# Stage 1 of a hybrid encoder layer: the normalized input taken by columns from memory, with the row factors spread by two transposes

## The chip, the cores and the metric

The kernel runs on one core of a Trainium2 chip. The metric is the device time of one execution in microseconds. The time before is the median of three runs; the profile is of one further execution.

## The reference

Two sequences (prompt and sample), each of 1024 rows and 1024 columns in fp32, go through one encoder layer. Each has a conditioning vector that modulates the normalized input:

```python
mod = jax.nn.silu(c) @ w_ada + b_ada
sh1, sc1, ga1, sh2, sc2, ga2 = split(mod, 6)
h = rmsnorm(x, g_mix) * (1.0 + sc1) + sh1      # rmsnorm: a factor for each row of x
z = h @ w_in                                   # q_lat 256, kv_lat 128, k_pe 64, f_in 512
y_mla = mla_group(q_lat, kv_lat, k_pe, ...)    # attention on low-rank latents, 4 heads
y_four = real(fft2(f_in)) per group @ w_four   # Fourier mixing
x = x + ga1 * (concat(y_mla, y_four) @ w_out)
h2 = rmsnorm(x, g_ffn) * (1.0 + sc2) + sh2
x = x + ga2 * ((silu(h2 @ w_gate) * (h2 @ w_up)) @ w_down)
y = rmsnorm(x, g_final)
```

Everything that the change touches lies in the first two lines of h and z.

## The kernel before

Every fp32 product is made of three matmuls (mm3, L78 to L80): each operand is split into a rounded part and a rest, by a cast on ACT (L62) and a subtraction on DVE (L63). A name ending in h (hh, eoh, lh) is the rounded part, one ending in l (hl, eol, ll) the rest.

Stage 1, which ends near 230 us, makes z in eight pairs k = 0 to 7, four for each sequence. A pair is two tiles of 128 rows (u = 0 and 1), rows p and p + 512, all 1024 columns. A program that schedules instructions places them; on each engine they then run in the fixed order that it chose, and SyncE's queue of loads and stores is in order too, at most eight under way at a time. For pair k, the code issues these steps:

- x_load(k+2): two loads of 512 KB into xt, the rows on partitions.
- zproj(k, 0): 24 matmuls make the 448 latent columns of tile 0 in a PSUM bank. ACT squares them (L413, L414), POOL makes the latents' row factors (rstd, L103 to L110: rs_v, rs_y, rs_w, rs_r), DVE makes the rotary products t (L420 to L422) and scales the latents into lat (L425, L426), POOL adds t into lat (L424), and the kv part is split and stored (ckv, L431).
- flip(k+1, 0) and flip(k+1, 1): h of the next pair by columns. Eight 128x128 transposes of xt on TensorE (L382) fill two banks; ACT multiplies by 1 + sc1 and adds sh1 (L389, hf; four pieces of 256 for these two flips, a few of pair 0 on DVE, L387), then hf is split into hh and hl, 512 at a time.
- zproj(k, 1), then latents(k, 0): four transposes of lat (L440), split into lh and ll and stored.
- flip(k+1, 2) and flip(k+1, 3): the other half of the columns.
- norm(k+2): ACT squares the rows of xt (L366), POOL makes the row factor rs_r by the same rstd, and DVE multiplies xt by it (L369).
- fourier_in(k, 0): 24 matmuls (F0 below) on the sum of the two tiles; latents(k, 1); evenodd(k+1, 0): POOL adds the two tiles of hf into eo (L400), which is split; fourier_in(k, 1) on the difference; evenodd(k+1, 1).

So zproj and fourier_in of pair k read what flip and evenodd made during pair k-1, and flip(k+1) reads what norm(k+1) made during pair k-1.

Between these steps a generator (extras) hands out other work: fold_out (a product of the output weights, L251, its result so on DVE, L253); eight products of 1 MB of modulation weights for the gates (mod_mm(1, c), L216, c = 0 to 7, "the second set", since the first eight for shift and scale are done before pair 0), each load (wada, L207) issued one step ahead; then gated output weights (L311, with so on DVE, L315). In pair 0 the flips stand behind zproj(0, 1) and among the products of fold_out.

The SBUF pool of the stage holds four xt tiles of 4 KB per partition and one hf tile of 8 KB per partition. The PSUM pool has eight banks, used in turn.

Of the kernel before, what the change touches and what calls it, by code (L numbers as in the profile page):

```python
# [21 lines left out]
P = 128  # L22
# [30 lines left out]
def hybrid_encoder_kernel(ctx: ExitStack, tc: tile.TileContext, a: dict):  # L53
# [109 lines left out]
    with ExitStack() as st:  # L163
# [5 lines left out]
        def bank():  # L169
            return pp.tile([P, 512], F32, tag="b", name="bank")  # L170

        def xtile():
            return w2.tile([P, D], F32, tag="x", name="xt", bufs=4)

# [26 lines left out]
        def wada_tile():  # L201
            return w2.tile([P, 4, 512], F32, tag="wada", name="wada", bufs=2)
# [149 lines left out]
        def x_load(k):  # L352
            s, j = pairs[k]
            st1["x", k] = [xtile() for _ in range(2)]
            for u in range(2):
                nc.sync.dma_start(st1["x", k][u], xs[s][rows(j, u), :])

        def norm(k):
            if ("x", k) not in st1:
                x_load(k)  # L360
            ms = tiny.tile([P, 2], F32, name="ms")
            xt = st1["x", k]
            for u in range(2):
                t = xt[u]
                jk = w.tile([P, D], BF16, tag="junk", name="junk", bufs=1)
                nc.scalar.activation(jk, t, AF.Square, scale=1.0 / 32.0, accum_out=ms[:, u : u + 1])  # L366
            r = rstd(ms, 2)
            for u in range(2):
                nc.vector.tensor_scalar(out=xt[u], in0=xt[u], scalar1=r[:, u : u + 1], scalar2=None, op0=ALU.mult)  # L369

        def flip(k, g):
            s, j = pairs[k]
            if g == 0:
                st1["hf", k] = w2.tile([P, NC, 2, P], F32, tag="hf", name="hf", bufs=1)
                st1["hh", k] = w.tile([P, NC, 2, P], F32R, tag=f"hh{k % 2}", name="hh")
                st1["hl", k] = w.tile([P, NC, 2, P], F32R, tag=f"hl{k % 2}", name="hl")
            hf, xt = st1["hf", k], st1["x", k]
            pt = bank().rearrange("p (c u t) -> p c u t", c=2, u=2)
            for c in range(2):
                for u in range(2):  # L380
                    cc = 2 * g + c
                    nc.tensor.transpose(pt[:, c, u, :], xt[u][:, cc * P : (cc + 1) * P], ident)  # L382
            for c in range(2):
# [95 lines left out]
        def wide(tag, shape=(P, 4, 512)):  # L479
            return (w2 if tag == "hf" else w).tile(list(shape), F32, tag=tag, name="wide")  # L480

# [39 lines left out]
        nc.sync.dma_start(ropes, a["ropes"])  # L521
        x_load(1)
        wpe = w.tile([P, 2, HEADS * ROPE], F32, tag="lh", name="wpe", bufs=2)
        nc.sync.dma_start(wpe, a["wpe"])
        wuvT = w.tile([P, HEADS, KVL], F32, tag="gah1", name="wuvT")
        nc.sync.dma_start(wuvT, a["wuvT"])
        wo2 = wo_load(0, wada_tile().rearrange("p a b -> p (a b)").rearrange("p (a b) -> p a b", a=2))
        mod_mm(0, 6, ch[6])
        wz_split(0, wz0)
# [9 lines left out]
        with behind():  # L539
            fold_pe(wpe, gq)  # L540
        zproj(0, 0)
        norm(1)
        evenodd(0, 1)
        nk = len(pairs)
        more = extras()

        def pair(k, also=None):
            if k + 2 < nk:
                x_load(k + 2)
            if also is not None:  # L550
                also(0)
            if k > 0:
                zproj(k, 0)
            if also is not None:
                with tc.issue_after(here["sq"]):
                    also(1)
            if 0 < k < nk - 1:
                flip(k + 1, 0)
                flip(k + 1, 1)
            next(more, None)  # L560
            zproj(k, 1)
            if k == 0:
                fold_out(0, wo2, wuvT, gq)
                flip(k + 1, 0)
                flip(k + 1, 1)
                fold_out(1, wo2, wuvT, gq)
# [1185 lines left out]
def _layout(i):  # L1752
# [10 lines left out]
    for s in range(2):  # L1763
# [3 lines left out]
    r = {  # L1767
        "x0": sq["x_prompt"][slots], "x1": sq["x_sample"][slots],
        "cT": c.reshape(2, NC, P).transpose(2, 1, 0),
        "w_ada": sq["w_ada"], "bT": b.reshape(48, P).T, "bga": bga,  # L1770
# [30 lines left out]
```

## Time and profile before

| | us |
|---|---|
| three runs | 2043.54, 2043.8, 2045.34 (median 2043.8) |
| the profiled execution | 2044.17 |
| its span, first to last instruction | 2042.3 |
| TensorE busy | 1986.2 (97%) |
| mean granted TensorE clock | 0.993 |

Stage 1 by stretches, each from the end of one pair's first projection to the next's (pair 1 ends its first projection at 85.87):

| stretch, us | length | TensorE busy | DVE | ACT | POOL | DMA share |
|---|---|---|---|---|---|---|
| 0 to 40 | 40.00 | 24.02 | 12.60 | 11.47 | 3.68 | 0.94 |
| 57 to 70 | 13.00 | 8.51 | 7.44 | 8.78 | 11.13 | 0.29 |
| 70 to 85.87 | 15.87 | 15.87 | 12.64 | 8.14 | 5.88 | 0.90 |
| 85.87 to 107.65 | 21.78 | 21.78 | 12.06 | 12.60 | 11.49 | 0.95 |
| 107.65 to 129.43 | 21.78 | 21.78 | 10.96 | 13.78 | 10.91 | 0.76 |
| 129.43 to 150.01 | 20.58 | 20.58 | 13.88 | 12.50 | 10.63 | 0.84 |
| 150.01 to 176.51 | 26.50 | 25.64 | 20.90 | 15.02 | 14.78 | 0.64 |
| 176.51 to 198.80 | 22.29 | 22.29 | 16.40 | 12.64 | 11.53 | 0.55 |
| 198.80 to 230 | 31.20 | 29.89 | 22.32 | 20.22 | 15.17 | 0.41 |

How to read the views: in a group, "a, b | c <-X d" is busy time, the mean in ns of one, and the idle time of that engine ahead of the group with what ended it. In a list of waits, the numbers are total, times and the longest. In a timeline, the numbers are start and duration; matmuls overlap, so their spacing is read from starts. In a row of windows, the columns are the length, busy time and count of TensorE, its weight loads, DVE, ACT and POOL, then the granted clock, the DMA share and GB/s.

### The profile page before, as it was taken

Reading aid. Unit: us, or ns where it says so; the run is one execution under the profiler, and the core shown is the slowest. Engines: PE = TensorE matmul, PEld = TensorE weight load, DVE = VectorE, ACT = ScalarE, POOL = GpSimd, SP = SyncE. Lnnn points to the kernel's source line nnn. Section 1 sums busy time; section 2 is a strip of 40 time slices with the busy share of each in tenths; the row PEclk is TensorE's granted clock in tenths of the full one; section 3 lists DMA queues with packets and bytes.
Section 4 is the critical chain, followed back from the end, with each engine's and each line's share of the span. In section 5 each row is a group of like instructions: output and inputs, shape, how many; then the busy total and the mean of one; then the engine's idle time right before and its main releaser. Section 6 shows DMA issues by size and latency. Waiting matters only on the chain.

```text
span 2042.3 us, 27832 instructions
## 1 busy us (share of the span) xinstructions
PE 1986.2 (97%) x9610; PEld 1629.8 (80%) x9610; DVE 1410.6 (69%) x2082; ACT 897.1 (44%) x1741; POOL 832.8 (41%) x1021
## 2 busy tenths in 40 slices
PE   6999999999999999999999999999999999999997
PEld 4788877888888877888888888877788888888876
DVE  3667757766677668878777676677766665657674
ACT  3655635555465554333333365453333333336441
POOL 0555213111313226879779410332654455410142
PEclk8999999999999999999999999999999999999999
DMA  9785694544643475546655587664423322358662
GB/s 358 237 257 180 224 337 133 126 104 103 160 114 128 125 273 196 191 164 202 202 164 191 179 306 249 215 232 146 140 101 103 109 98 103 113 182 271 231 217 90
DMA packets 183817, 370.30 MB, mean 181 GB/s; under 512 B 19004, under 2 KB 60476, under 8 KB 180604
## 3 DMA queue, kind: packets, MB, share of 16 engines
q1 hardware_dynamic: 165004, 310.72, 46.0%
q0 software_dynamic: 18672, 57.81, 9.5%
q8 instruction: 75, 1.23, 0.3%
q14 instruction: 66, 0.54, 0.1%
HBM read 256.46 MB, written 120.39 MB: 185 GB/s over the span
## 4 chain that ended last, share of the span: by engine, by line
PE 55%; DVE 3%; DMA 1%; POOL 1%; issue 1%; ACT 0%; SPq 0%; DVEq 0%; ACTq 0%; POOLq 0%
PE bank L79 18%; PE bank L78 18%; PE bank L80 18%; DVE wl L63 1%; DMA draw<-s_d 1%; DVE val L138 1%; ACT wh L62 0%; DMA val<-x_d 0%; DVE val L1600 0%; DMA rgu<-in_wgu_dram 0%; POOL val L138 0%; POOL rs_y L106 0%; DMA draw<-t_d 0%; SPq L1559 0%; DVE val L135 0%
## 5 line engine op out<-in xcount | busy, mean ns | idle before, releaser
L78 PE MATMUL bank<-H,wh 128*128 128x512 f32 x1224 | 477.4, 390 | 7.0 <-DVE val L138 6.5
L80 PE MATMUL bank<-H,wl 128*128 128x512 f32 x1224 | 476.5, 389 | 0.2 <-DVE wl L63 0.2
L79 PE MATMUL bank<-H,wh 128*128 128x512 f32 x1224 | 476.2, 389 | 0.0
L138 DVE TENSOR_TENSOR val<-bank,val 128x512 f32<-128x512 f32 x244 | 166.7, 688 | 167.4 <-PE bank L80 166.1
L78 PEld LDWEIGHTS bank<-H,wh 128*128 128x128 f32 x1224 | 229.8, 188 | 58.0 <-DVE val L138 7.7
L80 PEld LDWEIGHTS bank<-H,wl 128*128 128x128 f32 x1224 | 229.8, 188 | 49.1 <-DVE wl L63 1.5
L79 PEld LDWEIGHTS bank<-H,wh 128*128 128x128 f32 x1224 | 229.8, 188 | 47.4
L63 DVE TENSOR_TENSOR wl<-draw,wh 128x512 fp32r<-128x512 f32 x286 | 202.2, 740 | 86.3 <-ACT wh L62 86.0
L62 ACT CAST wh<-draw 128x512 fp32r<-128x512 f32 x286 | 168.9, 620 | 159.9 <-PE bank L79 85.3
L79 PE MATMUL bank<-wl,wh 128*128 128x512 f32 x572 | 223.7, 391 | 4.0 <-DVE wl L63 4.0
L138 POOL TENSOR_TENSOR val<-val 128x512 f32<-128x512 f32 x58 | 83.6, 1449 | 345.5 <-DVE val L1574 191.5
L78 PE MATMUL bank<-wh 128*128 128x512 f32 x572 | 222.7, 389 | 0.4 <-ACT wh L62 0.4
L80 PE MATMUL bank<-wh,wl 128*128 128x512 f32 x572 | 222.7, 389 | 0.0
L62 ACT CAST wh<-rgu 128x512 fp32r<-128x512 f32 x171 | 106.3, 623 | 251.0 <-PE bank L79 192.1
L63 DVE TENSOR_TENSOR wl<-val,wh 128x512 fp32r<-128x512 f32 x133 | 140.4, 1057 | 70.9 <-ACT wh L62 70.7
L63 DVE TENSOR_TENSOR wl<-rgu,wh 128x512 fp32r<-128x512 f32 x171 | 166.6, 975 | 7.3 <-ACT wh L62 7.2
L62 ACT CAST wh<-val 128x512 fp32r<-128x512 f32 x133 | 82.3, 622 | 179.9 <-PE bank L79 158.6
L135 POOL TENSOR_TENSOR val<-rgu 128x512 f32<-128x512 f32 x80 | 113.8, 1422 | 100.0 <-DMA rgu<-in_wgu_dram 96.3
L79 PEld LDWEIGHTS bank<-wl,wh 128*128 128x128 f32 x572 | 107.4, 188 | 29.4 <-DVE wl L63 7.3
L78 PEld LDWEIGHTS bank<-wh 128*128 128x128 f32 x572 | 107.4, 188 | 23.2 <-ACT wh L62 0.9
L80 PEld LDWEIGHTS bank<-wh,wl 128*128 128x128 f32 x572 | 107.4, 188 | 22.2
L135 POOL TENSOR_TENSOR val<-val 128x512 f32<-128x512 f32 x89 | 119.4, 1358 | 1.3
(381 smaller groups left out, 3913.2 us busy)
## 6 DMA issues: line engine op xcount, KB each, us to landing
rgu<-in_wgu_dram SPq DMA_DIRECT2D x86, 512.0 KB
draw<-s_d SPq DMA_DIRECT2D x143, 256.0 KB
s_d<-val POOLq DMA_DIRECT2D x88, 256.0 KB, 3.5
draw<-t_d SPq DMA_DIRECT2D x88, 256.0 KB
s_d<-val SPq DMA_DIRECT2D x66, 256.0 KB
draw<-in_w_down_dram SPq DMA_DIRECT2D x55, 256.0 KB
wada<-in_w_ada_dram SPq DMA_DIRECT2D x13, 1024.0 KB
xt<-in_x_dram SPq DMA_DIRECT2D x16, 512.0 KB
```

The source lines that it names most:

```text
L62: here["a"] = nc.scalar.copy(hi, src).ins
L63: here["v"] = nc.vector.tensor_tensor(out=lo, in0=src, in1=rd(hi), op=ALU.subtract).ins
L78: nc.tensor.matmul(out, lh, rh, start=first, stop=False, skip_group_check=cont)
L79: nc.tensor.matmul(out, lh, rl, start=False, stop=False, skip_group_check=cont)
L80: nc.tensor.matmul(out, ll, rh, start=False, stop=last, skip_group_check=cont)
L135: return eng.tensor_tensor(out=out, in0=x, in1=y, op=ALU.subtract).ins
L138: return eng.tensor_tensor(out=out, in0=x, in1=y, op=ALU.add).ins
```

## The change

From pair 1 on, h by columns no longer comes from transposes of xt. The host also gives x already laid out by columns (xT, 128 partitions of column index, 8 chunks, 2 tiles, 128 rows). A load of 1 MB (xT_load) puts it into hf, of which there are now two; xt is loaded still, for the squares alone, and has two tiles in place of four. The row factor has to multiply along the free axis there, so scale_cols spreads it: two transposes on TensorE of rs_r broadcast along columns (L383) give a 128x256 block in a PSUM bank whose every partition holds the factors of the 256 rows, and two DVE multiplications of 1024 elements (L386) scale hf in place. flip then runs ACT's multiply-add on hf in place (L410) and splits it as before. Pair 0 keeps its path.

Three things move with it. x_load(1) and xT_load(1) are issued behind wpe, wuvT and the first output weights. norm(1) is issued ahead of zproj(0, 0), and evenodd(0, 1) behind norm(1)'s last POOL operation. The load xT(k+2) fills the hf that pair k used, so on SyncE it waits until POOL has read that in evenodd(k, 1).

```diff
-            return w2.tile([P, D], F32, tag="x", name="xt", bufs=4)
+            return w2.tile([P, D], F32, tag="x", name="xt", bufs=2)
...
+        def xT_load(k):
+            s, j = pairs[k]
+            st1["hf", k] = w2.tile([P, NC, 2, P], F32, tag="hf", name="hf", bufs=2)
+            nc.sync.dma_start(st1["hf", k], a[f"xT{s}"][j])
...
             r = rstd(ms, 2)
+            if k > 0:
+                st1["r", k] = r
+                return
             for u in range(2):
                 nc.vector.tensor_scalar(out=xt[u], in0=xt[u], scalar1=r[:, u : u + 1], scalar2=None, op0=ALU.mult)
+
+        def scale_cols(k):
+            hf, r = st1["hf", k], st1.pop(("r", k))
+            pr = bank()[:, :256].rearrange("p (u t) -> p u t", u=2)
+            for u in range(2):
+                nc.tensor.transpose(pr[:, u, :], r[:, u : u + 1].broadcast_to([P, P]), ident)
+            for g in range(2):
+                gs = slice(4 * g, 4 * g + 4)
+                nc.vector.tensor_tensor(out=hf[:, gs], in0=hf[:, gs], in1=pr.unsqueeze(1).broadcast_to([P, 4, 2, P]), op=ALU.mult)
...
-            pt = bank().rearrange("p (c u t) -> p c u t", c=2, u=2)
-            for c in range(2):
-                for u in range(2):
-                    cc = 2 * g + c
-                    nc.tensor.transpose(pt[:, c, u, :], xt[u][:, cc * P : (cc + 1) * P], ident)
+            if k > 0:
+                pt = hf[:, 2 * g : 2 * g + 2]
+            else:
+                pt = bank().rearrange("p (c u t) -> p c u t", c=2, u=2)
+                for c in range(2):
+                    for u in range(2):
+                        cc = 2 * g + c
+                        nc.tensor.transpose(pt[:, c, u, :], xt[u][:, cc * P : (cc + 1) * P], ident)
...
-        x_load(1)
         wpe = w.tile([P, 2, HEADS * ROPE], F32, tag="lh", name="wpe", bufs=2)
...
         wo2 = wo_load(0, wada_tile().rearrange("p a b -> p (a b)").rearrange("p (a b) -> p a b", a=2))
+        x_load(1)
+        xT_load(1)
         mod_mm(0, 6, ch[6])
...
+        with behind():
+            norm(1)
+        placed = here["p"]
         zproj(0, 0)
-        norm(1)
-        evenodd(0, 1)
+        with tc.issue_after(placed):
+            evenodd(0, 1)
...
             if k + 2 < nk:
                 x_load(k + 2)
+                xT_load(k + 2)
...
             if 0 < k < nk - 1:
+                scale_cols(k + 1)
                 flip(k + 1, 0)
                 flip(k + 1, 1)
             next(more, None)
             zproj(k, 1)
             if k == 0:
                 fold_out(0, wo2, wuvT, gq)
+                scale_cols(k + 1)
                 flip(k + 1, 0)
```

The scheduler sets the rest. Two places of its order follow. The first is ACT in pair 2, from the squares of the first projection (L413 and L414, now L434 and L435) to those of the second. Before:

```order
L413 ACTIVATE junk,mz<-bank 128x256
L414 ACTIVATE junk,mz<-bank 128x128
L389 ACTIVATE hf<-bank,sh_0_77,s_0_75 128x256 x3
L62 CAST hh<-hf 128x512
L62 CAST kv<-lat 128x128
L389 ACTIVATE hf<-bank,sh_0_77,s_0_75 128x256
L62 CAST hh<-hf 128x512
L413 ACTIVATE junk,mz<-bank 128x256
```

In the changed kernel, where L410 is what L389 was:

```order
L434 ACTIVATE junk,mz<-bank 128x256
L435 ACTIVATE junk,mz<-bank 128x128
L410 ACTIVATE hf<-hf,sh_0_77,s_0_75 128x256 x3
L62 CAST kv<-lat 128x128
L62 CAST hh<-hf 128x512
L410 ACTIVATE hf<-hf,sh_0_77,s_0_75 128x256 x2
L62 CAST hh<-hf 128x512
L410 ACTIVATE hf<-hf,sh_0_77,s_0_75 128x256 x2
L434 ACTIVATE junk,mz<-bank 128x256
```

Three more hf stand ahead of the second squares, and kv ahead of the first hh.

The second is DVE in pair 6, up to the scaling of the first tile's latents (L425 and L426, now L446 and L447); t_2293, t_2197 and t_2265 are rotary products. Before:

```order
L420 TENSOR_TENSOR t_2293<-bank,ropec 128x64
L421 TENSOR_TENSOR t_2293<-bank,ropes 128x32
L422 TENSOR_TENSOR t_2293<-bank,ropes 128x32
L315 TENSOR_TENSOR so<-bank,gah 128x512
L63 TENSOR_TENSOR hl<-hf,hh 128x512 x2
L425 TENSOR_SCALAR lat<-bank,rs_r 128x256
L426 TENSOR_SCALAR lat<-bank,rs_r 128x128
```

In the changed kernel, behind the three operations of the first tile's t (t_2197); t_2265 is the second tile's:

```order
L386 TENSOR_TENSOR hf<-hf,bank 128x1024 x2
L315 TENSOR_TENSOR so<-bank,gah 128x512 x3
L63 TENSOR_TENSOR hl<-hf,hh 128x512 x2
L441 TENSOR_TENSOR t_2265<-bank,ropec 128x64
L315 TENSOR_TENSOR so<-bank,gah 128x512
L442 TENSOR_TENSOR t_2265<-bank,ropes 128x32
L443 TENSOR_TENSOR t_2265<-bank,ropes 128x32
L63 TENSOR_TENSOR hl<-hf,hh 128x512 x2
L315 TENSOR_TENSOR so<-bank,gah 128x512
L446 TENSOR_SCALAR lat<-bank,rs_r 128x256
L447 TENSOR_SCALAR lat<-bank,rs_r 128x128
```

The first tile's scaling now stands behind both L386, five so, four hl and the second tile's t.

On TensorE, the product of the second set moved too: the one for c = 0 runs behind zproj(1, 0), c = 1 within fourier_in(1, 1), c = 2 within zproj(2, 0), c = 3 within zproj(2, 1), and so on to c = 7 at the start of zproj(4, 0). On SyncE, the loads for c = 1, 2 and 4 stand behind an xT load and the stores of ckv or of the latents that follow it. From the end of pair 6 on, the order on every engine is as before.

More of the change, by code (lines that the diff above doesn't have):

```diff
@@ L373, in flip @@
             if g == 0:
-                st1["hf", k] = w2.tile([P, NC, 2, P], F32, tag="hf", name="hf", bufs=1)
+                if k == 0:
+                    st1["hf", k] = w2.tile([P, NC, 2, P], F32, tag="hf", name="hf", bufs=2)
                 st1["hh", k] = w.tile([P, NC, 2, P], F32R, tag=f"hh{k % 2}", name="hh")
@@ L479, in wide @@
         def wide(tag, shape=(P, 4, 512)):
-            return (w2 if tag == "hf" else w).tile(list(shape), F32, tag=tag, name="wide")
+            if tag == "hf":
+                return w2.tile(list(shape), F32, tag=tag, name="wide", bufs=2)
+            return w.tile(list(shape), F32, tag=tag, name="wide")
         cols0 = [(0, 2048)]
@@ L1768, in _layout @@
         "x0": sq["x_prompt"][slots], "x1": sq["x_sample"][slots],
+        **{f"xT{s}": x[slots].reshape(2, 4, P, NC, P).transpose(1, 4, 3, 0, 2)
+           for s, x in enumerate((sq["x_prompt"], sq["x_sample"]))},
         "cT": c.reshape(2, NC, P).transpose(2, 1, 0),
```

## The prediction

> **What bounds the kernel now.** I read the page first (busy shares and the chain that ended last), then TensorE's waits and line groups in stage 1, then timelines of single pairs.
>
> ```profile
> PE 1986.2 (97%) x9610; PEld 1629.8 (80%) x9610; DVE 1410.6 (69%) x2082; ACT 897.1 (44%) x1741; POOL 832.8 (41%) x1021
> PE 55%; DVE 3%; DMA 1%; POOL 1%; issue 1%; ACT 0%; SPq 0%; DVEq 0%; ACTq 0%; POOLq 0%
> ```
>
> TensorE works 97% of the span: a TensorE instruction taken out is worth its time, unless the next instruction then has to wait. Between 58 and 300 us, TensorE waits only here:
>
> ```profile
> PE bank L382 <- DVE xt L369: 4.5, 1, 4.5
> PE bank L440 <- DVE lat L425: 2.2, 3, 0.9
> PE bank L899 <- DMA wada<-in_w_ada_dram: 1.6, 1, 1.6
> ```
>
> The first is the first wait for a row factor, the second says that the latent chain is already just in time in three pairs. A steady pair on TensorE (pair 1, from the end of its first projection):
>
> ```profile
> 85.67 0.36 PE L80 MATMUL bank<-wz_h,hl 128*128 128x448 f32 x1
> 85.87 1.03 PE L382 MATMUL bank<-ident,xt 128*128 128x128 f32 x8
> 86.83 1.06 PE L216 MATMUL bank<-wada,scT 128*32 128x512 f32 x8
> 87.83 0.48 PE L78 MATMUL bank<-wz_h,hh 128*128 128x448 f32 x1
> 92.77 0.60 PE L440 MATMUL bank<-ident,lat 128*128 128x128 f32 x4
> 93.20 1.04 PE L382 MATMUL bank<-ident,xt 128*128 128x128 f32 x8
> 94.17 1.06 PE L216 MATMUL bank<-wada,scT 128*32 128x512 f32 x8
> 95.17 0.39 PE L78 MATMUL bank<-wcs_h,eoh 128*128 128x280 f32 x1
> ```
>
> By starts, eight transposes take 86.83 - 85.87 = 0.96 and 94.17 - 93.20 = 0.97 us, so 0.12 each; L440 takes 0.43, a 1 MB modulation product (L216) 1.00, the second projection 92.77 - 87.83 = 4.94. The chain beside it, from a projection's end to the scaled latents:
>
> ```profile
> 86.07 0.38 ACT L413 ACTIVATE junk<-bank 128x256 bf16<-128x256 f32 x1 [3.32 <-PE bank L80]
> 86.89 0.22 POOL L103 TENSOR_SCALAR rs_v<-mz 128x2 f32<-128x2 f32 x1 [5.01 <-ACT junk L414]
> 89.04 0.48 DVE L425 TENSOR_SCALAR lat<-bank,rs_r 128x256 f32<-128x256 f32 x1 [1.79 <-POOL rs_r L110]
> 89.44 0.34 DVE L426 TENSOR_SCALAR lat<-bank,rs_r 128x128 f32<-128x128 f32 x1
> ```
>
> 85.87 to 89.78: 3.9 us at best. Before, TensorE has 0.43 + 0.97 + 1.00 + F0 (3.1, the 24 matmuls from 95.17 at 0.13) = 5.5 us between zproj(k,1) and latents(k,1), which covers it.
>
> **The change part by part.** Prices of what it touches, from the line groups up to 340 us:
>
> ```profile
> L382 PE MATMUL bank<-ident,xt 128*128 128x128 f32 x128 | 19.0, 298 | 4.5 <-DVE xt L369 4.5
> L369 DVE TENSOR_SCALAR xt<-xt,rs_r 128x1024 f32<-128x1024 f32 x16 | 11.4, 751 | 12.7 <-POOL rs_r L110 12.7
> L63 DVE TENSOR_TENSOR ll<-bank,lh 128x512 fp32r<-128x512 f32 x16 | 10.9, 685 | 0.3
> L342 DVE TENSOR_TENSOR wcs_l<-bank,wcs_h 128x256 fp32r<-128x256 f32 x16 | 6.4, 421 | 12.5 <-ACT wcs_h L341 12.0
> L389 ACT ACTIVATE hf<-bank,sh,s 128x256 f32<-128x256 f32 x60 | 31.2, 576 | 8.4 <-PE bank L382 8.4
> L62 ACT CAST hh<-hf 128x512 fp32r<-128x512 f32 x32 | 20.0, 628 | 1.4 <-DVE hf L387 1.1
> L62 ACT CAST lh<-bank 128x512 fp32r<-128x512 f32 x16 | 9.2, 583 | 0.0
> ```
>
> Removed: 7 x 16 transposes of xt; added: 7 x 2 of rs_r. That is 14 x 0.12 = 1.69 us less in each of seven pairs, if nothing waits.
>
> L386 in place of L369: no trace has it. Below, L369's 0.75 us for 1024 elements; above, two 512-wide PSUM operations, 2 x 0.685 = 1.37. From 421 ns (256) to 685 (512) the step is 264 per 256 elements, so 685 + 2 x 264 = 1.21 us, which I take. It also stands after the first projection, directly ahead of the hf activations, where L369 was done early. The Trainium skill, "VectorE: DVE Perf Modes", section "Why PSUM operands drop a tier", says that fp32 work with a PSUM operand runs at the single rate while a single-source operation in SBUF can run at twice that. It speaks against this change; by it L386 is nearer 1.2 than 0.75, and at 0.75 the sum below would be about 1 us better, through pairs 1 and 6 alone. hf from SBUF instead of PSUM: hh (SBUF) against lh (PSUM) is 45 ns more at 512, so 0 to 0.05 each, taken as nothing; each runs beside projections.
>
> What stops the gain is the interval. Without the 0.97, and with the modulation product moved into or ahead of the projections, TensorE reaches latents(k,1) 0.43 + 3.1 = 3.5 us after zproj(k,1), against a chain of 3.9. ACT adds to it: in pairs 1 to 3 seven hf, two hh and kv stand ahead of the second squares, where four hf, two hh and kv stood. Starting when L386 and the first squares are through (about 1.6 us after the projection), three hf take 1.4 us, kv waits for lat to 4.0, then kv 0.2, hh 0.5, two hf 0.95, hh 0.5, two hf 0.95: the second squares start at 7.15. Spacings are by starts, a little under the means above.
>
> Pair by pair, after minus before, against the profiled execution:
>
> - Pair 0: the 4.5 us stall is shown by
>
> ```profile
> 65.55 0.41 PE L382 MATMUL bank<-ident,xt 128*128 128x128 f32 x2 [4.49 <-DVE xt L369]
> 62.20 0.22 POOL L103 TENSOR_SCALAR rs_v<-ms 128x2 f32<-128x2 f32 x1
> 64.65 1.42 DVE L369 TENSOR_SCALAR xt<-xt,rs_r 128x1024 f32<-128x1024 f32 x2 [1.31 <-POOL rs_r L110]
> ```
>
>   The factor now comes at about 60, ahead of zproj(0,0)'s own, and 1.9 us of transposes go. In exchange POOL makes lat(0,0) and lat(0,1) behind it and behind two eo, so latents(0,0) waits in its place. fourier_in(0,0) comes at about 70.3 in place of 72.6: -2.4 (bounds -1 to -3.5).
> - Pair 1: L386 is held up behind pair 0's last so (L253) and splits; latents(1,1) waits about 2.0: 2.0 - 1.69 = +0.3. The third modulation product waits 0 to 2 us for its load, which now goes out behind xT(3) and ckv writes; taken 0.3. Together +0.6.
> - Pairs 2 and 3: zproj(k,1) ends at 0.24 + 4.9 + 1.0 = 6.2, squares at 7.15, lat at 10.9; TensorE is there at 9.7 to 9.9. A wait of 1.0 leaves -0.75 each, -1.5.
> - Pair 4: only four hf stand ahead of the squares, and the 0.86 of the latent waits goes: -1.69 - 0.86 = -2.55.
> - Pair 5: lat(5,0) on DVE stands behind work of zproj(5,1): +0.4 after the gain.
> - Pair 6: the largest term. Before:
>
> ```profile
> 198.80 1.03 PE L382 MATMUL bank<-ident,xt 128*128 128x128 f32 x8
> 204.42 0.47 DVE L425 TENSOR_SCALAR lat<-bank,rs_r 128x256 f32<-128x256 f32 x1
> 205.03 0.63 PE L440 MATMUL bank<-ident,lat 128*128 128x128 f32 x4 [0.39 <-DVE lat L425]
> 205.50 1.04 PE L382 MATMUL bank<-ident,xt 128*128 128x128 f32 x8
> ```
>
>   lat(6,0) starts 5.6 us after the projection's end and fourier_in(6,0) 7.6. After, ahead of lat(6,0) on DVE stand two L386 (2.4), five so (5 x 0.6), four hl (2.4) and six small t (0.6), 8.4 us, and the last hl needs an hh that ACT makes only behind the second squares. lat at about 10.8, fourier_in at 11.6: +4.1 (bounds +1 to +5).
> - Pair 7: the latent wait at 227 (0.9) shrinks: -0.8.
>
> The sum is -2.4 + 0.6 - 1.5 - 2.55 + 0.4 + 4.1 - 0.8 = -2.2 us.
>
> The clock: TensorE then stands still about 5.5 us in pair 6. What a stall does to it, in windows of 5 us:
>
> ```profile
> 60.00:65.00 5.00, 1.06 (x3) 0.19 (x1) 2.10 (x7) 3.51 (x10) 4.09 (x14) 1.00 0.26 75
> 65.00:70.00 5.00, 4.45 (x14) 2.66 (x15) 2.99 (x9) 2.68 (x7) 4.21 (x12) 0.66 0.21 63
> 155.00:160.00 5.00, 4.14 (x25) 2.21 (x23) 3.79 (x15) 3.64 (x12) 3.40 (x10) 1.00 0.41 113
> ```
>
> Behind the 4.5 us stall the clock is 0.66 over 5 us, 1.7 us of work lost; behind the 0.86 us stall of 156 it stays 1.00. For 5.5 us I take 1.7, between 0 and 1.7. The total is -0.5: 2044.17 - 0.5 = 2043.7. The profiled execution is 2044.17 (span 2042.3 and 1.9 around it), 0.4 above the median of 2043.8.
>
> Loads: seven more of 1 MB. In windows, one of the loading at the start and two pairs:
>
> ```profile
> 35.00:40.00 5.00, 1.09 (x12) 0.16 (x8) 1.93 (x6) 2.48 (x5) 0.00 (x0) 0.89 1.02 421
> 85.87:107.65 21.78, 21.78 (x146) 18.03 (x144) 12.06 (x27) 12.60 (x32) 11.49 (x26) 1.00 0.95 292
> 107.65:129.43 21.78, 21.78 (x146) 18.03 (x144) 10.96 (x25) 13.78 (x34) 10.91 (x26) 1.00 0.76 237
> ```
>
> At 421 GB/s (1.02 of the engines busy) one takes 2.5 us, at 292 (0.95) 3.6. Pairs 1 and 2 stand at 0.95 and 0.76 of 21.8 us; 2.5 more is 0.11 each, 1.06 and 0.87: pair 1 is just over, and the gap at 60 to 70 (0.26 and 0.21 busy) now takes x(2), which before went out at 48. I cost it at the 0.3 above. xT(k+2) waits on SyncE until POOL has read hf in evenodd(k,1); behind it stand ckv and latent writes, and the modulation loads, which TensorE waits for. If that cover goes, it is the third rival.
>
> **The rivals.**
>
> 1. The queue in pair 6 does not bite: if ACT's hh comes early enough and so runs before lat's factor is ready, lat(6,0) starts near its old 5.6 us and pair 6 gains its 1.69 instead of losing 4.1 and 1.7. That is 7.5 us better: 2036.2. For it: DVE has idle time between all these (12 us busy of 21.8 above). Against it: DVE works in order, and 8.4 us stand ahead of lat by count. Chance 0.29. If no pair waits for lat at all, -2.4 - 6 x 1.69 - 0.86 - 0.4 - 0.8 = -14.6, so 2029.6; against it speaks 3.5 against 3.9. Chance 0.05.
> 2. Slower through the loads: where xT's wait and its 2.5 us push a modulation load past its place on TensorE's list, the product (L216) waits, up to 2.5 us each at the second, third, fifth, sixth and eighth product of the second set. At four of these it adds 10: 2053.7. It decides when a load lands more than its margin late, by my count 2 us for the second, none for the third, 1.5 to 4 for the others. For it: 0.95 busy. Against: no wait for wada between 58 and 300 us before, save one at L899. Chance 0.16.
> 3. Slower through the clock: the waits of pair 0, 1 and 6 each end in a half-clock window, and pair 6's order costs its upper bound: -2.2 + 0.9 + 3 x 1.7 = +3.8, with pair 1's upper bound of 2 us on the load +5.5: 2049.7. Chance 0.12. The Trainium skill, "TensorE: Matmul & The Clock Gate", Part 1, has a free-running window of 3413 ns, one idle window giving half rate until a busy one; the rows above agree in both cases.
>
> That the change does not do what it says (transposes out, time not) is the forecast itself, the likeliest, with 0.38.
>
> **How the numbers follow.** 0.2% (4.1 us) is about what a measurement of this kernel can tell from no change. Faster: rival 1, 0.29 + 0.05 = 0.34. Same: the forecast, 0.38. Slower: rivals 2 and 3, 0.16 + 0.12 = 0.28. The forecast's own range is 2040 to 2047.5: pair 0 (-1 to -3.5), pair 6's bounds and the clock. The range for 8 in 10 reaches to 2035.5, which takes in rival 1's likelier half, and to 2051, which takes in rival 3 and the light half of rival 2; left out are the full gain and rival 2 at full price, together about 0.15 to 0.2.
>
> **What would show it.** Right: TensorE's waits list L440 <- DVE lat in pairs 1 to 3 with 1 to 2 us each and in pair 6 with about 5.5; L382's 4.5 is gone, a latent wait stands in pair 0; L386 takes 1.2 us; fourier_in(0,0) starts near 70.3; the groups of L79 and L80 after 300 us are unchanged in time. Wrong: latent waits under 0.5 us in all pairs (rival 1), waits of L216 on wada (rival 2), granted clock under 1.00 after 70 us in more than one window (rival 3), or a change behind stage 1.

## The result: 2056.5 us, slower by 0.6%, outside the predicted range

The changed kernel takes 2056.51 us (median of 5, 2053.62 to 2059.49) beside 2043.54 us for the kernel before (median of 5, 2042.95 to 2045.34). The ratio is 1.0059, with an interval of 1.0048 to 1.007. The forecast was 2043.7 with a range up to 2051.0. One of the eleven executions of run e9 below took 4011.76 us; its ratio leaves that one out, and without it its median is 2042.8.

The profiled execution is the longest of the five: 2059.49, span 2057.7, clock 0.988; the shortest, 2053.62, had 0.993. So the profile shows 15.4 us more span (2057.7 - 2042.3) where the medians show 13.0. The first operation of the stage behind stage 1 starts at 249.54 us in place of 231.00: stage 1 costs 18.5. Behind it the waits are 4.6 us shorter in all (15.9 in place of 20.5) and one more half-clock window takes 1.7 back, and 18.5 - 4.6 + 1.7 = 15.6. The work behind stage 1 is unchanged. The cause is therefore to be looked for in stage 1.

The page of the changed kernel, first part: TensorE has 98 matmuls fewer (14 x 7) and 6 us more of busy time.

```profile
PE 1992.2 (97%) x9512; PEld 1622.1 (79%) x9512; DVE 1415.1 (69%) x2082; ACT 900.5 (44%) x1741; POOL 833.2 (40%) x1021
```

By pairs, as stretches from the end of one first projection to the next; each difference is after minus before:

| pair | first projection ends, before | after | difference, measured | predicted |
|---|---|---|---|---|
| 0 | 85.87 | 83.05 | -2.8 (-0.6 of it ahead of pair 0) | -2.4 |
| 1 | 107.65 | 111.51 | +6.7 | +0.6 |
| 2 | 129.43 | 134.42 | +1.1 | -0.75 |
| 3 | 150.01 | 157.24 | +2.2 | -0.75 |
| 4 | 176.51 | 181.07 | -2.7 | -2.55 |
| 5 | 198.80 | 211.07 | +7.7 | +0.4 |
| 6 and 7, to the next stage | 231.00 | 249.54 | +6.3 | +5.0 (4.1 + 1.7 - 0.8) |

(The row of pair k gives the end of pair k+1's first projection.) Pairs 0, 4, 6 and 7 came as predicted within 1.3 us; pairs 1 and 5 together are 13 us worse, 2 and 3 together 5.

TensorE's waits between 58 and 300 us (total, times, longest):

```profile
PE bank L461 <- DVE lat L446: 15.8, 5, 6.2
PE bank L78 <- DVE lat L447: 0.8, 1, 0.8
PE bank L929 <- DMA wada<-in_w_ada_dram: 0.8, 1, 0.8
PE bank L251 <- DVE so L253: 0.8, 1, 0.8
```

The 4.5 us wait for xt is gone and latents stand in its place: 15.8 us in five waits against 2.2 in three. No product of the second set (L216) waits for its load. The four that count, in the timeline of TensorE (start, duration, and in brackets the wait), are in pairs 0, 1, 5 and 6:

```profile
65.59 0.63 PE L461 MATMUL bank<-ident,lat 128*128 128x128 f32 x4 [1.62 <-DVE lat L446]
...
96.04 1.09 PE L461 MATMUL bank<-ident,lat 128*128 128x128 f32 x4 [2.92 <-DVE lat L446]
...
191.11 0.69 PE L461 MATMUL bank<-ident,lat 128*128 128x128 f32 x2 [4.85 <-DVE lat L446]
...
222.45 1.32 PE L461 MATMUL bank<-ident,lat 128*128 128x128 f32 x4 [6.19 <-DVE lat L446]
```

Pairs 2 and 3 have none. Instead, the products of the second set are torn in two. Pair 2 on TensorE, behind its first projection:

```profile
113.13 0.36 PE L79 MATMUL bank<-wz_l,hh 128*128 128x448 f32 x1
113.42 1.05 PE L216 MATMUL bank<-wada,scT 128*32 128x512 f32 x4
114.41 0.47 PE L80 MATMUL bank<-wz_h,hl 128*128 128x448 f32 x1
114.72 0.37 PE L78 MATMUL bank<-wz_h,hh 128*128 128x448 f32 x1
114.92 0.37 PE L79 MATMUL bank<-wz_l,hh 128*128 128x448 f32 x1
115.22 1.05 PE L216 MATMUL bank<-wada,scT 128*32 128x512 f32 x4
116.20 0.47 PE L80 MATMUL bank<-wz_h,hl 128*128 128x448 f32 x1
```

A whole product, x8 in the rows of before, took 1.00 us by starts. Here half of one takes 114.41 - 113.42 = 0.99 and the other half 116.20 - 115.22 = 0.98. The group over stage 1, of before and then of after, has the same 64 rows:

```profile
L216 PE MATMUL bank<-wada,scT 128*32 128x512 f32 x64 | 8.5, 605 | 0.0
```

```profile
L216 PE MATMUL bank<-wada,scT 128*32 128x512 f32 x64 | 16.7, 635 | 0.0
```

8.2 us more, of which 6.9 are the splitting of seven products (7 x 0.98) and the rest is half clock. That is more than half of what the transposes gave back: 14 x 0.12 x 7 = 11.8. For three of the seven the trace shows when the load of the second half landed (issued at 91.27, 103.98 and 141.46, landed after 6.9, 7.0 and 5.2 us): each was there before even the first half began (98.34, 113.42 and 150.96). These three at least need not have been split when they ran.

The third part is the clock. Of the windows of 5 us, those around the last three waits above (length, the busy time of each engine, then clock, DMA share, GB/s):

```profile
95.00:100.00 5.00, 3.96 (x14) 2.29 (x14) 4.59 (x9) 4.08 (x9) 3.63 (x10) 0.51 0.50 191
100.00:105.00 5.00, 5.00 (x28) 3.69 (x27) 1.55 (x4) 0.54 (x2) 3.62 (x4) 0.80 1.00 233
190.00:195.00 5.00, 3.89 (x8) 1.16 (x10) 3.02 (x10) 3.10 (x10) 4.31 (x11) 0.57 0.68 230
195.00:200.00 5.00, 5.00 (x23) 2.74 (x20) 1.59 (x4) 0.66 (x2) 0.18 (x1) 0.75 0.99 359
220.00:225.00 5.00, 2.55 (x11) 2.21 (x12) 3.82 (x9) 1.83 (x5) 3.67 (x8) 0.64 0.42 141
225.00:230.00 5.00, 5.00 (x30) 5.00 (x30) 0.81 (x3) 1.12 (x3) 0.00 (x0) 0.68 0.48 131
```

(1 - clock) x 5 summed gives 3.45, 3.4 and 3.4: 10.25 us of TensorE time, where before lost 1.7 in all of stage 1.

In sum, for stage 1: -11.8 for the transposes; +10.7 for waits (17.35 in place of 6.66, which is the 4.5 for xt and the 2.2 for latents); +6.9 for split products; +8.5 for the clock. Together that is +14.3, and some 4 us of the 18.5 are assigned to no row.

### The profile page after: what moved, and what is told of

It reads as the page before. It is cut to its first block, busy times and chain, and to the rows that moved or that the text cites. A ratio compares the mean times of both kernels' runs of the same rounds, so it can differ in the third digit from the quotient of the medians.

```text
span 2057.7 us, 27636 instructions
## 1 busy us (share of the span) xinstructions
PE 1992.2 (97%) x9512; PEld 1622.1 (79%) x9512; DVE 1415.1 (69%) x2082; ACT 900.5 (44%) x1741; POOL 833.2 (40%) x1021
## 3 DMA queue, kind: packets, MB, share of 16 engines
q8 instruction: 74, 1.21, 0.2%
## 4 chain that ended last, share of the span: by engine, by line
PE 54%; DVE 2%; DMA 2%; issue 1%; POOL 1%; ACT 0%; SPq 0%; DVEq 0%; ACTq 0%; POOLq 0%
PE bank L79 18%; PE bank L78 18%; PE bank L80 18%; DVE wl L63 1%; DMA val<-x_d 1%; DMA draw<-s_d 1%; DVE val L138 1%; POOL val L138 0%; DMA draw<-t_d 0%; ACT wh L62 0%; DVE val L1630 0%; DVE val L135 0%; SPq L1589 0%; SPq L1590 0%; DVE val L1526 0%
```

## The experiments

Three theories stood behind the result. S: the products are split because their loads come late, and the halves cost. W: the latents wait because h of the next pair is ahead of them on DVE and ACT. C: what the waits cost is doubled by the clock. A fourth, Q, came out of the first four runs: SyncE's in-order queue, which the seven xT loads joined, is behind both. "Next stage at" is the start of the first operation behind stage 1 in the profile (before 231.00, after 249.54); it is the sharper number, since nothing that was edited lies behind it and the rest of the span differs by up to 7 us between these profiles (1805.6 us in e9, 1812.2 in e11). It is one execution of each kernel all the same: for after the slowest of its five, for e9 and e10 the fastest of theirs. For each run the scheduler set the order anew, so more than the edit can differ.

| run | next stage at | median (n) | before beside it | ratio, interval |
|---|---|---|---|---|
| after | 249.54 | 2056.51 (5) | 2043.54 | 1.0059, 1.0048 to 1.007 |
| e1_whole | 243.23 | 2050.44 (11) | 2044.21 | 1.0029, 1.0018 to 1.0039 |
| e2_hold | 252.98 | 2058.78 (5) | 2044.21 | 1.0071, 1.0056 to 1.0085 |
| e3_whole_hold | 241.66 | 2052.05 (8) | 2044.21 | 1.0038, 1.0025 to 1.005 |
| e4_before_split | 237.91 | 2050.38 (9) | 2044.21 | 1.0031, 1.0021 to 1.004 |
| e5_pool_queue | 237.78 | 2047.77 (11) | 2044.34 | 1.0013, 1.0003 to 1.0023 |
| e6_pool_whole | 236.56 | 2048.12 (11) | 2044.34 | 1.0012, 1.0003 to 1.0022 |
| e7_before_early | 230.84 | 2043.9 (11) | 2044.34 | 0.9993, 0.9982 to 1.0003 |
| e8_warm | 242.62 | 2054.44 (5) | 2044.34 | 1.0048, 1.0035 to 1.0061 |
| e9_queues | 228.54 | 2043.2 (11) | 2044.84 | 0.9992, 0.9981 to 1.0003 |
| e10_queues_whole_hold | 225.93 | 2036.94 (5) | 2044.84 | 0.9958, 0.9944 to 0.9972 |
| e11_fill0 | 227.25 | 2040.82 (8) | 2044.01 | 0.9984, 0.9973 to 0.9996 |
| e12_queues_whole | 227.34 | 2039.09 (12) | 2044.01 | 0.9975, 0.9962 to 0.9987 |

### Products that cannot be split (e1), and the kernel before with split ones (e4)

In e1 the weights of a product come by one load of 1 MB in place of two of 512 KB:

```diff
 def mod_load(c, cols, wt):
+    if len(cols) == 2:
+        nc.sync.dma_start(
+            wt.rearrange("p (t j) n -> p t (j n)", t=2),
+            a["w_ada"][c * P : (c + 1) * P, :].rearrange("p (t n) -> p t n", n=D)[:, 2::3, :])
+        return wt
```

> The changed kernel, with each 1 MB of gate weights loaded by one transfer in place of two halves, so that the four matmuls of a product of the second set (L216) stand together again on TensorE; nearly nothing else moves. Theory S (the products split into halves cost the time: 4 matmuls of 32 output columns each took 1.0 us together, two halves take 0.98 each): seven products get about 1.0 us shorter, 7 us in all, 2049.5, and the group of L216 falls from 16.7 to about 8.5 us. Theory W (waits for the latents and the clock windows behind them are all of it): no change, 2056. Theory L (the seven loads more): the bytes are the same, no change.

All products stay whole. Their group falls from 16.7 to 8.9, the next stage starts 6.3 us earlier, and the median falls by 6.1 (the edit moves lines down by five: L221 is L216, L466 and L451 are L461 and L446):

```profile
L221 PE MATMUL bank<-wada,scT 128*32 128x512 f32 x64 | 8.9, 629 | 0.0
```

Not all of the 7.8 arrives, since TensorE now waits 18.3 us for the latents where it waited 15.8. Two of these waits, 0.78 and 1.51 us, are in pairs 2 and 3, where the changed kernel had none. No whole product waits for its load.

```profile
PE bank L466 <- DVE lat L451: 18.3, 7, 6.2
```

e4 is the other way about: the kernel before, with the second half of seven products put later by hand, behind other matmuls.

```diff
-            for j in range(4):
-                nc.tensor.matmul(...)
+            half((0, 1) if key == 1 and c > 0 else range(4))
+            if key == 1 and c > 0:
+                late.append(lambda: half((2, 3)))
```

> The kernel before, with the second half of seven products of the second set put twelve matmuls later, into the middle of the next projection or Fourier product; every other engine's order is as before but for two rows. Theory S: seven times 0.98, 6.9 us more, 2050.4, and the L216 group doubles from 8.5 to about 16 us. Theories W and L: no change, 2043.5.

```profile
L220 PE MATMUL bank<-wada,scT 128*32 128x512 f32 x64 | 15.8, 605 | 0.0
```

The group grows by 7.3 and the next stage starts 6.9 later, with about the same waits (4.4 and 1.3) and the same clock; the median is 6.2 above before. Split products cost 1 us each whichever kernel they stand in. This settles S as to the price.

### Holding h of the next pair back (e2, e3)

e2 lets the first two flips' splits go out only behind the scaled latents, and the other two behind the second squares, so that on DVE the hl of the first two no longer stands ahead of lat. e3 does this and e1's edit.

```diff
+                with tc.issue_after(here["lat"]):
+                    flip(k + 1, 0)
+                    flip(k + 1, 1)
...
+                with tc.issue_after(here["sq"]):
+                    flip(k + 1, 2)
+                    flip(k + 1, 3)
```

> The changed kernel, with the splits of the first two flips queued behind the first tile's scaled latents on DVE, and ACT's work of the last two flips behind the second squares; TensorE's and SyncE's orders are as in the changed kernel. Theory W: pair 1's wait of 2.9 us goes to about 1, with it the half-clock window behind it (3.4 us), pair 5's 4.9 falls by about 1.5 and pair 6's 6.2 by about 1.5, since the five so stay ahead there: 6 to 8 us less, about 2049.5. Theory S: no change, 2056, and the L216 group stays at 16.7 us. Theory L: no change.

> Both edits of the two runs above. If S and W both hold, they add: 13 to 15 us less than the changed kernel, 2041.5 to 2043.5, about the kernel before. If only one holds, 2049. What stays of the loss against the kernel before less the 11.8 us of transposes is then the waits of pairs 5 and 6 with their half-clock windows.

Both missed. In e2 the wait of pair 1 falls from 2.92 to 1.79, but pair 5 has 5.20 and pair 6 has 6.86, in sum about as much as in after, and the three half-clock stretches cost 3.4, 5.1 and 5.1, 13.6 us in place of 10.25:

```profile
PE bank L461 <- DVE lat L446: 15.7, 5, 6.9
```

e3 keeps the two long waits, 5.33 and 6.86, and 10.25 us of half clock, and ends 1.6 us of stage 1 better than e1 and no better in the median. W as it was stated, hl ahead of lat, therefore holds for the wait of pair 1 (though in e2 that pair as a whole is 1.0 us longer) and is not the cause in pair 5, where in e2 no hl stands ahead of lat. In pair 6 of e2 the hl of the last two flips still do, at 222.65 and 223.81 with lat at 225.69, so there W is not tested. DVE in pair 5 of the changed kernel shows more; the first projection ends at 181.07, where the transposes of the factor (L383) start:

```profile
182.17 0.69 DVE L315 TENSOR_TENSOR so<-bank,gah 128x512 f32<-128x512 f32 x1 [1.82 <-DMA wm_d<-so]
184.19 0.69 DVE L315 TENSOR_TENSOR so<-bank,gah 128x512 f32<-128x512 f32 x1 [1.34 <-DMA wm_d<-so]
184.80 1.21 DVE L386 TENSOR_TENSOR hf<-hf,bank 128x1024 f32<-128x1024 f32 x1
...
190.59 0.47 DVE L446 TENSOR_SCALAR lat<-bank,rs_r 128x256 f32<-128x256 f32 x1
```

Two gated output weights (so) stand ahead of L386, and each waits until an earlier so has been stored from its tile, 1.82 and 1.34 us. so and lat take their tiles from one ring of three (sk). So L386 starts 3.7 us behind the projection, everything behind it moves along, and lat starts 9.5 us behind it. In before, lat stood at 179.75 for a projection that ended at 176.51, 3.2 us, since DVE had only one so and the rotary products between. Of the 6.3 us more, 3.2 are the two waits; the rest is the order, with both L386, one more so, two hl and part of the second tile's t ahead of lat. No run takes these two apart, and a larger ring was not tried. In pair 6 DVE waits for no store: there the order alone puts lat 10.85 us behind the projection (221.92 for 211.07).

### The seven loads off SyncE's queue (e5, e6)

The stores of so, and the loads of the products, stand on SyncE's queue behind the xT loads. SyncE in pair 1, before (the first product's load there, L207, starts at 85.85) and after, where xt and xT go ahead of it:

```profile
85.85 2.55 SPq L207 DMA_DIRECT2D wada<-in_w_ada_dram  x2
```

```profile
87.77 0.42 SPq L356 DMA_DIRECT2D xt<-in_x_dram  x1
88.29 0.41 SPq L361 DMA_DIRECT2D hf<-in_xT_dram  x1
89.55 1.03 SPq L452 DMA_DIRECT2D ckv_d<-kv  x2
90.68 1.27 SPq L207 DMA_DIRECT2D wada<-in_w_ada_dram  x2
```

An xT load itself hardly waits in the queue, 0.2 us at the longest between 60 and 230 us. The long waits are those of the ckv stores for ACT's kv, and the loads of the products now stand behind such stores. SyncE's waits for kv from 84 to 150 us, in before, in after and in e9 (below):

```profile
SPq L431 <- ACT kv L62: 8.9, 6, 2.7
```

```profile
SPq L452 <- ACT kv L62: 30.1, 6, 8.8
```

```profile
SPq L452 <- ACT kv L62: 11.3, 5, 2.9
```

The last of the product loads goes out at 141.02 in place of 127.42, and the last product ends near 154 in place of 139. e5 has POOL issue the xT loads from pair 3 on, e6 also has whole products.

```diff
-            nc.sync.dma_start(st1["hf", k], a[f"xT{s}"][j])
+            (nc.gpsimd if k > 2 else nc.sync).dma_start(st1["hf", k], a[f"xT{s}"][j])
```

> The changed kernel, with one edit: from pair 3 on, the 1 MB load by columns is issued by POOL, whose own read of that hf it waits for, in place of SyncE's queue. Theory Q (in SyncE's in-order queue that load holds the modulation loads and the stores of so behind it; from that come the split products, the late so and the late latents of pairs 5 and 6): three of the products stay split, the L216 group falls from 16.7 to about 11.5 us (5 us less); the waits of pairs 5 and 6 (4.9 and 6.2) fall under 2 each, 7 us less, and their half-clock windows (3.4 each) go: 19 us less, about 2037. Theory D (DVE alone is too full there with two L386 and the so): the waits stay, only the L216 part comes, 2051. If the bytes themselves are too many (theory L), the loads late on POOL's queue show as waits of L386 or hf on DMA, and the time stays at 2050 or above.

> POOL's queue for the loads by columns from pair 3 on, and each gate weight load whole, so no product is split. Against the run with POOL's queue alone theory S wants 3 us less (three products of 1 us): 2034 if theory Q holds, 2046 if theory D holds.

Half of it came: the next stage starts 11.8 us earlier, only two products have other matmuls between their halves (two more run in two pieces because the second half waits for its load, 0.24 and 0.87 us), and pairs 5 and 6 wait 0.16 and 3.0 us in place of 4.85 and 6.19. In pair 5 no so and nothing of the second tile stands ahead of lat any more (lat itself waits 1.93 us for a store of so). The median is 2047.8 where 2037 was expected. But a new wait has come up in pair 1:

```profile
PE bank L216 <- DMA wada<-in_w_ada_dram: 7.5, 3, 6.4
PE bank L461 <- DVE lat L446: 4.3, 4, 2.3
```

The product that waits 6.4 us, at 97.41, has its load issued at 88.69 and 92.29; ahead of it on SyncE, at 87.85, stands the second row load of xt for pair 3, which has two xt tiles in place of four to go to. The window behind this wait has half clock too. In e6 the whole products do not help (next stage at 236.56, 6.2 us of waits for wada). So the row loads were taken off the queue as well, which is e9.

### The early factor alone (e7)

In e7 the kernel before takes only the early norm(1) and evenodd(0, 1) behind it, for the 4.5 us wait of pair 0.

```diff
+        with behind():
+            norm(1)
+        placed = here["p"]
         zproj(0, 0)
-        norm(1)
-        evenodd(0, 1)
+        with tc.issue_after(placed):
+            evenodd(0, 1)
```

> The kernel before, with only the part on pair 0: norm(1) ahead of zproj(0, 0), evenodd(0, 1) behind its last POOL operation; x_load(1) stays where it was and everything later too. The changed kernel came 2.8 us earlier to the end of pair 1's first projection, 0.6 of it from the start-up, and 1.9 us of that pair's transposes are still here: between 0 and 2.2 us less than before, 2042, if the latent wait takes the stall's place in part; if the whole 4.5 us stall goes, 2039 with 1.7 of it by the half-clock window.

The long wait is gone, and with it the half clock (1.00 from 65 to 70, where before had 0.66):

```profile
60.00:65.00 5.00, 3.90 (x17) 2.17 (x16) 2.75 (x5) 0.91 (x2) 4.55 (x8) 1.00 0.13 47
65.00:70.00 5.00, 2.56 (x11) 1.05 (x10) 2.94 (x10) 4.75 (x13) 4.18 (x15) 1.00 0.09 26
```

Yet the next stage starts 0.2 us earlier and the median does not move (0.9993). In place of one wait stand several, 1.2 for lat, 1.1 for xt, 1.1 more for lat and 0.5 for hf; together they are 0.6 us shorter than what they replace, and 1.7 us of half clock are gone. But the first projection of pair 0 ends 2.3 us later than in before (ACT squares it at 58.87 in place of 56.58), 1.1 of it ahead of that projection, and this takes the gain back; why it is later stays open. By itself, then, the early factor is not shown to gain anything.

### Keeping TensorE busy in the waits (e8)

e8 is the changed kernel with 22 and 28 matmuls of no use behind the second projections of pairs 5 and 6, where it waits 4.85 and 6.19 us. They fill the waits and compute nothing that is read.

```diff
+            if k in (5, 6):
+                keep_warm(22 if k == 5 else 28)
```

> The changed kernel, with 22 and 28 matmuls (448 columns, 0.2 us each, into a bank that nobody reads) put behind the second projections of pairs 5 and 6, where TensorE waits 4.9 and 6.2 us. They do no useful work. Theory C (each long wait costs 3.4 us more by the clock): the clock stays 1.00 in pairs 5 and 6, 6.8 us less, 2049.7. If the low clock only follows something else (the pair's loads, say), it stays and the time is 2056 or a little more.

The clock stays at 1.00 behind both, and the next stage starts 6.9 us earlier:

```profile
190.00:195.00 5.00, 4.16 (x23) 2.41 (x24) 4.25 (x12) 3.22 (x8) 4.67 (x11) 1.00 0.80 270
195.00:200.00 5.00, 5.00 (x34) 3.45 (x34) 2.25 (x4) 3.10 (x7) 0.13 (x1) 1.00 1.00 340
220.00:225.00 5.00, 5.00 (x43) 5.00 (x42) 2.75 (x5) 2.22 (x5) 0.22 (x1) 1.00 0.62 169
```

Pair 5 is 3.2 us shorter, pairs 6 and 7 are 2.8, near the 3.4 each that the rows of after showed. The other 1.0 lies ahead of them, where nothing was edited: there pair 1 waits 2.64 us and loses 1.7 us of clock, in place of 2.92 and 3.45. So in stage 1 the clock's part is shown for pairs 5 and 6. In the whole time less of it arrives: the span of the profiled execution is 5.0 shorter, the median 2.1, with intervals that overlap after's. The other executions of the changed kernel had a clock of 0.990 to 0.993 against the 0.988 of the profiled one, so the three stretches need not all be in each of them.

### Both kinds of load off the queue (e9, e10, e12)

e9 moves the xT loads from pair 2 on to POOL and the row loads from pair 3 on to ACT. e12 adds e1's whole products, e10 these and e2's hold.

```diff
-                nc.sync.dma_start(st1["x", k][u], xs[s][rows(j, u), :])
+                (nc.scalar if k >= 3 else nc.sync).dma_start(st1["x", k][u], xs[s][rows(j, u), :])
...
-            nc.sync.dma_start(st1["hf", k], a[f"xT{s}"][j])
+            (nc.gpsimd if k >= 2 else nc.sync).dma_start(st1["hf", k], a[f"xT{s}"][j])
```

> The changed kernel, with one kind of edit: the loads by columns from pair 2 on are issued by POOL and the row loads from pair 3 on by ACT (which does the squares that they wait for), so that SyncE's queue holds neither. In the run with POOL's queue alone, the loads of the gate weights still stood behind the second row tile of pair 3 and one product waited 6.4 us for its load in pair 1. Theory Q: no product is split (the order has all eight whole), the wait of 6.4 us in pair 1 falls under 1, and its half-clock window goes: 3 + 6 + 3.4 us less than that run, about 2036. Theory L (too many bytes in pairs 0 to 2 whatever the queue): products still wait 3 us or more for weights there, 2044 to 2048.

> The same two queues, the gate weights in whole loads, and the splits and ACT's work held behind the latents and the second squares. If theories Q and W both hold, the latent waits of pairs 1 to 3 are under 1 us too: 2 to 3 us less than with the queues alone, 2033. If the whole load of 1 MB comes later than its first half did, a product waits about 1 us each in pairs 1 and 2 and it is the same time.

> Both queues and whole loads, without the held work; TensorE's order is that of the run with all three. Theory W (hl and hf ahead of latents and squares cost time): the latent waits of pairs 1 to 3 come back with 1 to 2 us each where ACT reaches the second squares late, 3 to 5 us more than with the held work, 2041. If holding does nothing once the loads are out of SyncE's queue, 2037; the difference to the queues alone (2043.2) is then what the whole loads give.

With no other edit than which engine issues these loads, and the order that follows from it, e9 brings the next stage from 249.54 to 228.54, ahead of before's 231.00. The bytes are the same, so these were not too many (theory L). In the order no product is split; one still runs in two pieces, since its second half waits 1.4 us for its load (the group takes 9.6 us in place of 16.7). TensorE's waits nearly halve:

```profile
PE bank L461 <- DVE lat L446: 7.9, 7, 3.8
PE bank L216 <- DMA wada<-in_w_ada_dram: 1.4, 1, 1.4
```

e9's profiled execution is 2035.85, its fastest; over all, its median is 2043.2, no different from before (0.9981 to 1.0003) and 7 us above what was expected. Whether the order of the queue alone does it, or also that SyncE has at most eight loads and stores under way, is not taken apart. e10 does better, 2036.94 (2033 expected), and beats both kernels: 0.9958 of before, with an interval wholly below 1, and 19.6 us below the changed kernel. Its waits up to 300 us:

```profile
PE bank L466 <- DVE lat L451: 7.9, 6, 3.8
PE bank L221 <- DMA wada<-in_w_ada_dram: 1.1, 1, 1.1
```

e12, without the hold, has 0.9975 with an interval that overlaps e10's: whether the hold helps here stays open. That whole products add to the queues is not separated cleanly either (0.9992 and 0.9975, intervals that overlap between 0.9981 and 0.9987).

### The last long wait (e11)

e10's longest wait, 3.8 us, is in pair 0, and has half clock behind it. e11 fills it with 18 matmuls of no use.

```diff
+                keep_warm(18)
                 with tc.issue_after(here["sq"]):
                     flip(k + 1, 2)
                     flip(k + 1, 3)
```

> The run with both queues, whole loads and held work, with 18 matmuls of no use (0.2 us each, 3.6 in all, into a bank that nobody reads) in pair 0, where TensorE waits 3.8 us for the first latents. Theory C (a wait of that length starts a low-clock stretch that costs 3.4 us, and busy time prevents it): the clock stays 1.00 from 60 to 80 us, 3.4 us less, 2033.5, unless the 18 end later than the latents come. If the clock follows something else, no change or a little more, 2037.

Missed. The clock is 1.00 at 65 to 70 in place of 0.70, but TensorE, at its next work only 0.4 us sooner (68.18 in place of 68.59), then waits 2.8 us for so (L258), and the half clock comes behind that:

```profile
65.00:70.00 5.00, 4.95 (x23) 3.54 (x22) 2.52 (x6) 1.77 (x6) 3.30 (x13) 1.00 0.74 241
...
75.00:80.00 5.00, 5.00 (x21) 4.04 (x20) 5.00 (x7) 4.08 (x9) 1.30 (x1) 0.68 0.91 288
```

The next stage starts 1.3 us later than in e10. The stall had moved to the next late operand, and the fill gained nothing.

## Why the prediction was wrong, and where it was right

**Right.** Pair 0: -2.8 against -2.4, with fourier_in(0,0) at 69.80 against the 70.3 foreseen. Pair 4: -2.7 against -2.55. Pair 6, with pair 7: +6.3 against +5.0, with lat 10.85 us behind the projection against 10.8 and a wait of 6.19 against 5.5. L386 took 1.213 us, against the estimate of 1.21. That agrees with the single rate for an fp32 operation with a PSUM operand, of which "VectorE: DVE Perf Modes" of the Trainium skill speaks ("Why PSUM operands drop a tier"); whether the PSUM operand or the second input slows it against L369's 0.75, no run here shows:

```profile
L386 DVE TENSOR_TENSOR hf<-hf,bank 128x1024 f32<-128x1024 f32 x14 | 16.8, 1213 | 9.4 <-PE bank L383 9.3
```

Behind stage 1 the work did not change. The main mechanism, TensorE early and the latents late, was right; the sum was not.

**Wrong, first: the price of a product.** Pairs 2 and 3 were costed with "zproj(k,1) ends at 0.24 + 4.9 + 1.0 = 6.2", one product of 1.00 us each. In the changed kernel seven products run in halves, of which the prediction says nothing. A half costs 0.98 us, nearly as much as the whole. So 6.9 us in pairs 1 to 3 were left out, and in pairs 2 and 3, where TensorE came later for it, they took the place of the waits that had been foreseen: those pairs had no wait, and still lost 1.1 and 2.2 against the -0.75 each. In e1, with whole products, the waits are there, 0.78 and 1.51 against the 1.0 each. The row of before that priced a product was a row of four matmuls side by side and said nothing of two by themselves.

**Wrong, second: rival 2's way.** The rival expected waits of L216 for its load, 2053.7, with a chance of 0.16. There are none. The loads do go out later, but they cost time in another way: in the fixed order of the changed kernel seven products, whose weights come in two loads each, stand in two pieces, and this turns up as busy time of TensorE. e1 (one load, no split), and e5 and e9 (loads off the queue, two such splits and none) tie the splits to the loads. That the scheduler reckoned the second loads late is an inference; when the kernel ran, at least three of them were in time. What the profile was to show of it, waits of L216, could not have shown it.

**Wrong, third: pair 5.** It was taken at "+0.4 after the gain", for lat behind the work of the second projection. The term was too small for that order, and it left out so's wait for its store (L315, 3.2 us in two waits), which came ahead of L386. This was visible in part: in the prediction, so was counted on DVE as 0.6 us of work in pair 6, without asking which tile it writes. Measured +7.7: a wait of 4.85, 3.4 of half clock, less the 1.69, and 1.1 that no row explains.

**Wrong, fourth: the clock.** It was taken at 1.7 us, once, in pair 6, from the one stall of before. Measured 3.4 in each of pairs 1, 5 and 6, and in pair 1 behind a wait of 2.92 us that was costed at 2.0 without any. Of the 13 us by which pairs 1 and 5 were missed, 6.8 are this. Rival 3 had the clock (three windows of 1.7) and came to 2049.7, but each of its windows was half of what was measured.

The waits together came to 17.35 us. The prediction has 2.0 + 1.0 + 1.0 + 5.5 for pairs 1, 2, 3 and 6, and one in pair 0 without a size; so what it missed of the waits is above all pair 5's 4.85.

## What to carry to other kernels

A load added to an in-order queue is priced by what then stands behind what in that queue, not by its own 2.5 us: with the loads issued by other engines and no other edit, the same kernel was 13 us faster. When a schedule is made anew, look at what has been torn apart in it, since work that ran side by side may cost double in two places, and then shows as busy time and not as a wait. And price a stall of TensorE of 2 us or more with its clock: in this kernel it cost between nothing and 5.1 us on top, most often 3.4.

## What the runs showed of the hardware

**Matmuls of 32 columns run side by side only when they stand together.** Four of them (weights 128x32, 512 wide, fp32) take 1.00 us from start to start, two 0.98. The Trainium skill, "TensorE: Matmul & The Clock Gate", Part 3, "Packing small matmuls — row/col tiling", says that matmuls on different column tiles run concurrently, with 2.38x for three of them. The rows here agree as far as they go, since four take the time of two (no row shows one by itself), and e4 adds what it costs to place other matmuls between: 7.3 us for seven products.

**The clock's loss came in steps, and the length of a wait does not give their number.** In the profiles the loss up to 500 us, (1 - clock) x length, was 10.3 (before, e4, e8 and e10), 12 (e9), 18.8 (e1 and e2) and 20.5 (after): steps of about 1.7 us. Behind single waits, from windows of 5 us, it was 5.1 (5.20 and 6.86 us, e2), 3.4 (4.85 and 6.19 us, after) and 1.7 (4.49 us, before). At one place in pair 1 it was 3.45 for 2.92 us (after), 1.7 for 2.64 (e8), nothing for 2.17 (e3), and yet 3.4 for 1.79 (e2, with a further wait of 0.79 close behind). In pair 6 a wait of 1.94 us cost 1.7 in e9 and nothing in e12. The same page of the Trainium skill, Part 1, has a free-running window of 3413 ns; half rate for one such window is 1.7 us, which is the step here. It wants a whole window idle before the rate falls. The waits of 1.79 to 2.92 us that cost steps were shorter than a window, so the measurement decides against that as it stands; whether sparse work around a wait counts as idle too, and where the windows lie, no run here shows.
